# Four edits to the order of work in a hybrid conv/mLSTM decoder block: low weight products one block behind, gate columns first, a merge block in another head, and mean subtractions tile by tile

## The chip, the cores and the metric

The kernel runs on one core of a Trainium2 chip. The core has a matrix engine (TensorE, PE in the profile), whose weight loads the profile lists apart as PEld, a vector engine (VectorE, DVE), a scalar engine (ScalarE, ACT), a small general engine (GpSimd, POOL) and a sync engine (SyncE, SP) that issues most of the transfers. The engines run side by side, each through its own fixed list of instructions in order, and wait for each other through semaphores.

The metric is the device time of one execution in microseconds (us). The time of the kernel before is the median of three runs, 1705.99 us (1705.5 to 1708.39).

## The reference, cut to what matters

One decoder block over 1024 tokens of width 1024, in float32. A conditioned RMS norm feeds one wide input projection. Its columns go to a gated convolution branch, an mLSTM branch with four heads, and two merge gates per channel. The gated sum goes through an output projection, and a SwiGLU feed-forward network and a last norm follow.

```python
h = rms_norm(x, norm_mix_g[l]) * (1.0 + sc1) + sh1
proj = jnp.einsum("bsd,de->bse", h, w_in[l]) + b_in[l]
glu_in, qk_in, v, o_pre, if_pre, merge_pre = jnp.split(proj, IN_SPLITS, axis=-1)

a = glu_in[..., :CONV_WIDTH] * jax.nn.sigmoid(glu_in[..., CONV_WIDTH:])
a = causal_depthwise_conv(a, conv_dw_w[l], conv_dw_b[l])          # 31 taps
a = jax.nn.silu(layer_norm(a, conv_ln_g[l], conv_ln_b[l]))
y_conv = jnp.einsum("bsc,cd->bsd", a, w_conv_pw[l]) + b_conv_pw[l]

qk = jax.nn.silu(causal_depthwise_conv(qk_in, qk_conv_w[l], qk_conv_b[l]))   # 4 taps
...
hm = mlstm_chunkwise(heads(q), heads(k) * (MLSTM_HEAD_DIM ** -0.5), heads(v),
                     gates[:, :MLSTM_HEADS], gates[:, MLSTM_HEADS:])
...
y_mlstm = jax.nn.sigmoid(o_pre) * hm
g_conv, g_mlstm = jnp.split(jax.nn.sigmoid(merge_pre), 2, axis=-1)
y = jnp.einsum("bsd,de->bse", g_conv * y_conv + g_mlstm * y_mlstm, w_out[l])
x = x + g1 * y
...
x = x + g2 * jnp.einsum("bsf,fd->bsd", jax.nn.silu(gt) * up, w_ffn_down[l])
```

## The kernel before, in words

**Products.** Activations are kept transposed, 128 channels by 1024 tokens per tile. A float32 operand is split into a high part (written by ScalarE in the matmul's own 32-bit type) and a low part (the rest, subtracted by VectorE). A product is then three matmuls: high by high, high weights by low activations, low weights by high activations. One **block** is 128 output columns of a projection over the contraction of 1024, that is, over eight slices k of 128. `mm_k` (L160 to L165) issues, for one k, three products times two halves of 512 tokens: six matmuls, all recorded under L165. A block is 48 of them and writes one accumulator `mm` (two PSUM banks, two such tiles exist). `load_split` loads a block's weights `wraw` (512 KB, issued by SP), splits them into `whi` on ScalarE (L155) and `wlo` on VectorE (L156); each of the three has two buffers. `wblock` runs a block as a generator, one k per step, and `block` runs one at once for the pointwise convolution.

**Who sets the order.** The program is laid out as Python generators; a planner with a timing model then fixes each engine's list, by the program's order as priority, and lets work that is ready in the model pass work that isn't. `tc.high_priority()` moves instructions ahead in that priority. `queue_behind` adds an edge for the planner alone, which keeps one instruction behind another; on one engine it adds no wait at run time. `pump` hands out convolution taps (L395, VectorE, 31 for each of eight channel tiles) from a list `bg`, at a later priority, as credit comes in: each block gives 5500 of credit, a tap costs 1200.

**The stages around the change.** After a prologue (about the first 60 us) the first two gated convolution tiles g0 and g1 are made. For head 0, `v_part(0)` makes the value projection and, in the same matmuls, the eight columns of the input and forget gates: three tiles `wide` (pool tag `t4`, three buffers, shared with the sigmoids of `glu_gate`, `om` and `merge_conv`) hold the high value weights in columns 0 to 255, the high gate columns in 256 to 263 and the low ones in 264 to 271. L583 and L584 write those gate columns from the small load `wif_raw`. Then for each head: `qk_part` (four blocks with a 4-tap convolution on VectorE, L542, each), `v_part`, `decay_mask`, and `mlstm`, a chain over four chunks of 256 tokens that passes from TensorE to VectorE and ScalarE and back at each step and yields 22 times. `mix` weaves other blocks between its steps: `FILL[h]` names them, `NEXT[h]` says how many of their steps go first, and `STEPS[h]` how many follow each step of the chain. There g2 to g7 are convolution tiles (two blocks each), "o" is `om` of the head before (four blocks: two output gates and two merge gates), and m0 and m1 are the first two merge gates of the convolution branch (`merge_conv`, one block each, whose sigmoid is stored to DRAM as `mc_d` by a transfer on ScalarE's queue and loaded again when it is needed).

After head 3 come `om` of head 3, the sum over the channel tiles (`ln_sum`), and the layer norm of the convolution branch (`ln_steps`) woven with the merge blocks m2 to m7, two block steps after each of its steps. `ln_steps` makes the mean on TensorE in two halves of 512 tokens (L839), subtracts it (L844, VectorE, eight tiles times two halves), squares each tile on ScalarE (L846), adds the squares up (L848), and later writes the normalised tiles as `ah` and `al` (L864, L865). The pointwise convolution reads these. It is followed by the output projection, the second norm, and the feed-forward network, whose code the change doesn't touch.

## Time and profile before

| what | us |
|---|---|
| median of the three runs | 1705.99 |
| the profiled execution's own time | 1706.31 |
| its span, first to last instruction | 1704.6 |
| what lies around the span (1706.31 - 1704.6) | 1.71 |
| TensorE busy in the span | 1664.8 |
| VectorE busy in the span | 1310.5 |
| ScalarE busy in the span | 647.5 |

The profile shows one execution, taken by the hardware profiler. The busy time of TensorE counts the time in which at least one matmul is recorded as running. Matmuls are pipelined and their ends are modelled, so two neighbours overlap in the records, and the spacing of their starts tells the pace. A row of the timeline gives the start, the duration, the engine, the line, the operation, the tile written and the tiles read; in brackets stands the idle time of the engine just ahead of the row and what ended it. Rows of windows give the length of each stretch, then each engine's busy time in it with the number of instructions, then the TensorE clock that was granted (1.00 is full), the share of the DMA engines and the rate in GB/s.

### The profile page before, as it was taken

Reading aid. Unit: us, or ns where it says so; the run is one execution under the profiler, and the core shown is the slowest. Engines: PE = TensorE matmul, PEld = TensorE weight load, DVE = VectorE, ACT = ScalarE, POOL = GpSimd, SP = SyncE. Lnnn points to the kernel's source line nnn. Section 1 sums busy time; section 2 is a strip of 40 time slices with the busy share of each in tenths; the row PEclk is TensorE's granted clock in tenths of the full one; section 3 lists DMA queues with packets and bytes.
Section 4 is the critical chain, followed back from the end, with each engine's and each line's share of the span. In section 5 each row is a group of like instructions: output and inputs, shape, how many; then the busy total and the mean of one; then the engine's idle time right before and its main releaser. Section 6 shows DMA issues by size and latency. Waiting matters only on the chain. (4 is left out here: it accounts for less than half of the span.)

```text
span 1704.6 us, 20805 instructions
## 1 busy us (share of the span) xinstructions
PE 1664.8 (98%) x8237; PEld 1394.9 (82%) x8237; DVE 1310.5 (77%) x1760; ACT 647.5 (38%) x835; POOL 59.5 (3%) x116
## 2 busy tenths in 40 slices
PE   5999999999999999999999999999999999999998
PEld 4798888888888889888888778888888888788886
DVE  6989998997699759637699567877767777667776
ACT  7425335322532253224521356422222222344344
POOL 0000001000000000000000000000000000000001
PEclk9999999999999999999999999999999999999999
DMA  9221121122112211224497543333332333495872
GB/s 325 64 63 49 38 62 38 50 62 75 38 39 73 62 38 50 75 82 155 129 374 283 189 160 130 112 105 100 99 104 93 101 98 110 144 355 188 283 248 110
DMA packets 221241, 211.12 MB, mean 124 GB/s; under 512 B 8455, under 2 KB 175127, under 8 KB 221143
## 3 DMA queue, kind: packets, MB, share of 16 engines
q1 hardware_dynamic: 202327, 164.70, 31.3%
q10 hardware_dynamic: 18576, 44.31, 6.9%
q8 instruction: 64, 1.05, 0.3%
q0 software_dynamic: 240, 0.79, 0.1%
q14 instruction: 34, 0.28, 0.0%
HBM read 168.60 MB, written 41.16 MB: 123 GB/s over the span
## 5 line engine op out<-in xcount | busy, mean ns | idle before, releaser
L395 DVE SCALAR_TENSOR_TENSOR cacc<-a,col,cacc 128x1024 f32<-128x1024 f32 x240 | 306.1, 1282 | 3.9 <-ACT cacc L393 1.4
L165 PE MATMUL mm<-hh,wlo 128*128 128x512 f32 x864 | 271.2, 391 | 1.6 <-DVE wlo L156 1.6
L165 PE MATMUL mm<-hl,whi 128*128 128x512 f32 x864 | 272.5, 392 | 0.0
L165 PE MATMUL mm<-hh,whi 128*128 128x512 f32 x864 | 271.6, 392 | 0.0
L165 PEld LDWEIGHTS mm<-hh,wlo 128*128 128x128 f32 x864 | 160.4, 188 | 33.7 <-DVE wlo L156 2.8
L165 PEld LDWEIGHTS mm<-hl,whi 128*128 128x128 f32 x864 | 161.0, 188 | 32.1 <-issue 0.5
L165 PEld LDWEIGHTS mm<-hh,whi 128*128 128x128 f32 x864 | 160.5, 188 | 31.6
L155 ACT ACTIVATE whi<-wraw 128x1024 fp32r<-128x1024 f32 x61 | 64.7, 1060 | 227.4 <-PE mm L165 176.1
L156 DVE TENSOR_TENSOR wlo<-wraw,whi 128x1024 fp32r<-128x1024 f32 x61 | 74.3, 1219 | 28.7 <-ACT whi L155 25.2
L1123 PE MATMUL mm<-Bh,gh 128*128 128x512 f32 (+1 forms) x192 | 71.5, 375 | 2.8 <-ACT gh L1060 1.4
L1124 PE MATMUL mm<-Bl,gh 128*128 128x512 f32 (+1 forms) x192 | 71.5, 373 | 0.7 <-DVE Bl L1042 0.7
L611 PE MATMUL mm<-wlo,hh 128*128 128x256 f32 x256 | 72.0, 282 | 0.0
L1125 PE MATMUL mm<-Bh,gl 128*128 128x512 f32 (+1 forms) x192 | 71.2, 371 | 0.0
L1215 ACT ACTIVATE wd<-reg 128x1024 fp32r<-128x1024 f32 (+1 forms) x36 | 35.2, 988 | 82.6 <-DVE reg L1339 54.2
L542 DVE SCALAR_TENSOR_TENSOR cacc<-qkraw,col,cacc 128x1024 f32<-128x1024 f32 x48 | 61.5, 1281 | 4.9 <-ACT cacc L540 4.5
L1366 PE MATMUL mm<-wd,xl 128*128 128x512 f32 (+1 forms) x154 | 59.6, 387 | 1.2 <-DVE xl L1347 1.2
L1365 PE MATMUL mm<-wd,xh 128*128 128x512 f32 (+1 forms) x154 | 59.6, 387 | 0.0
L1367 PE MATMUL mm<-wd,xh 128*128 128x512 f32 (+1 forms) x154 | 59.5, 386 | 0.0
L610 PE MATMUL mm<-whi,hh 128*128 128x256 f32 x192 | 54.5, 284 | 0.0
L612 PE MATMUL mm<-whi,hl 128*128 128x256 f32 x192 | 54.2, 283 | 0.0
L1347 DVE TENSOR_TENSOR xl<-xr,xh 128x1408 fp32r<-128x1408 f32 x27 | 43.7, 1619 | 8.7 <-ACT xh L1346 8.7
L1216 DVE TENSOR_TENSOR wd<-reg,wd 128x1024 fp32r<-128x1024 f32 (+1 forms) x36 | 40.2, 1132 | 11.2 <-ACT wd L1215 11.0
(501 smaller groups left out, 3863.8 us busy)
## 6 DMA issues: line engine op xcount, KB each, us to landing
wraw<-in_w_in_dram SPq DMA_DIRECT2D x64, 512.0 KB
xr<-act_d SPq DMA_DIRECT2D x27, 704.0 KB
awt<-in_w_ada_dram SPq DMA_DIRECT2D x32, 512.0 KB
graw<-in_w_ffn_up_dram SPq DMA_DIRECT2D x24, 512.0 KB
act_d<-cg ACTq DMA_DIRECT2D x48, 256.0 KB
uraw<-in_w_ffn_up_dram SPq DMA_DIRECT2D x22, 512.0 KB
reg<-in_w_ffn_down_dram SPq DMA_DIRECT2D x20, 512.0 KB
other<-in_w_ffn_down_dram SPq DMA_DIRECT2D x20, 512.0 KB
```

What stands on the lines that cost most here:

```text
L155: nc.scalar.activation(hi, raw, AF.Copy)
L156: (eng or nc.vector).tensor_sub(lo, raw, hi.bitcast(F32))
L165: nc.tensor.matmul(flat(acc)[:, a:b], lhs[:, k, :], rhs[k][:, a:b], start=(first and k == 0), stop=(last and k == kt - 1))
L395: nc.vector.scalar_tensor_tensor(acc, a[:, j:j + S], dw_col(j, ct), acc, op0=OP.mult, op1=OP.add)
L542: nc.vector.scalar_tensor_tensor(cv, raw[:, j:j + S], wcol(j), cv, op0=OP.mult, op1=OP.add)
L611: nc.tensor.matmul(o[:, 0:256], hh[k][:, ts_], los[k], start=False, stop=False)
L1123: nc.tensor.matmul(o, a, rh, start=(k == 0), stop=False)
L1124: nc.tensor.matmul(o, a, rl, start=False, stop=False)
L1125: nc.tensor.matmul(o, b, rh, start=False, stop=(k == 3))
L1365: nc.tensor.matmul(o, xh, wh, start=(k == 0), stop=False)
L1366: nc.tensor.matmul(o, xl, wh, start=False, stop=False)
L1367: nc.tensor.matmul(o, xh, wl, start=False, stop=(k == FP - 1))
```

## The change

Four edits, none of which changes what is computed or how many matmuls there are.

1. `mm_k` issues the two matmuls with the low weights of slice k after the four with the high weights of slice k+1. In the last slice, those of k=6 and k=7 both follow. This holds for all blocks that go through `wblock` and `block`.
2. In `v_part(0)` the writes of the gate columns are put at high priority.
3. The merge block m1 moves from the fill of head 3 to the end of the fill of head 0, and head 0's pace goes from 1.8 to 2.1 block steps for each step of its chain.
4. In `ln_steps` the sixteen subtractions of the mean are kept in the program's order: both halves of tile 0, both of tile 1, and so on.

```diff
-STEPS = (1.8, 2.8, 2.8, 2.8)
+STEPS = (2.1, 2.8, 2.8, 2.8)
...
     def mm_k(acc, k, kt, w, xh, xl, parts=HALVES):
         hi, lo = w
-        for lhs, rhs, first, last in ((hi, xh, True, False), (hi, xl, False, False), (lo, xh, False, True)):
+        steps = [(hi, xh, k), (hi, xl, k)]
+        if k:
+            steps.append((lo, xh, k - 1))
+        if k == kt - 1:
+            steps.append((lo, xh, k))
+        for i, (lhs, rhs, j) in enumerate(steps):
             for a, b in parts:
-                nc.tensor.matmul(flat(acc)[:, a:b], lhs[:, k, :], rhs[k][:, a:b],
-                                 start=(first and k == 0), stop=(last and k == kt - 1))
+                nc.tensor.matmul(flat(acc)[:, a:b], lhs[:, j, :], rhs[j][:, a:b],
+                                 start=(k == 0 and i == 0), stop=(i == 3))
...
-                nc.vector.tensor_copy(t[:, 0:n, 256:264], wif_raw[:, ks])
-                nc.vector.tensor_sub(t[:, 0:n, 264:272], wif_raw[:, ks], t[:, 0:n, 256:264].bitcast(F32))
+                with tc.high_priority():
+                    nc.vector.tensor_copy(t[:, 0:n, 256:264], wif_raw[:, ks])
+                    nc.vector.tensor_sub(t[:, 0:n, 264:272], wif_raw[:, ks], t[:, 0:n, 256:264].bitcast(F32))
...
-    FILL = ("g2 g3 m0", "g4 o g5", "g6 o g7", "o m1")
+    FILL = ("g2 g3 m0 m1", "g4 o g5", "g6 o g7", "o")
...
         ssum = t4()
+        before = None
         for ct in range(8):
             for i in range(2):
-                nc.vector.tensor_sub(halves(cv[ct], i), halves(cv[ct], i), mean[i])
+                ins = nc.vector.tensor_sub(halves(cv[ct], i), halves(cv[ct], i), mean[i])
+                if before:
+                    queue_behind(ins, before)
+                before = ins
```

## The prediction

> **What bounds the kernel now.** The first view is the page's head: TensorE is busy 98% of the span. The second is the table of windows over stages, whose first figure after each stretch's length is TensorE's busy time.
>
> ```profile
> span 1704.6 us, 20805 instructions
> PE 1664.8 (98%) x8237; PEld 1394.9 (82%) x8237; DVE 1310.5 (77%) x1760; ACT 647.5 (38%) x835; POOL 59.5 (3%) x116
> ```
>
> ```profile
> 0.00:60.00 60.00, 42.19 (x194) 33.52 (x195) 46.47 (x73) 43.54 (x68) 2.74 (x8) 0.94 0.78 250
> 60.00:860.00 800.00, 795.32 (x4245) 683.83 (x4244) 644.92 (x842) 297.52 (x361) 40.24 (x89) 1.00 0.23 68
> 860.00:1100.00 240.00, 231.52 (x1204) 193.85 (x1203) 188.41 (x298) 102.14 (x154) 5.50 (x8) 1.00 0.60 206
> ```
>
> The change keeps every matmul, so it can win only idle time of TensorE. Its edits lie between 60 and 860 us, from the work ahead of head 0 to the end of the layer norm; only the blocks of the pointwise convolution, which edit 1 touches too, run on after that. There TensorE idles 800.00 - 795.32 = 4.7 us. The prologue (17.8 us) and the stage from 860 to 1100 (8.5 us) idle more, but no wait there is one of an edited line. The third view is the list of TensorE's waits in that stretch: what waited, what released it, us in total, times, the longest.
>
> ```profile
> PE pc L636 <- DVE kwl L684: 1.8, 1, 1.8
> PE mm L165 <- DVE wlo L156: 1.6, 2, 0.9
> PE mm L610 <- DVE t L584: 0.6, 1, 0.6
> PE pa L132 <- DVE col L135: 0.4, 1, 0.4
> PE pc L634 <- ACT kwh L683: 0.3, 1, 0.3
> ```
>
> That is 4.7 us, the whole idle time, in six waits. The first three kinds and the last belong to edits 3, 1, 2 and 3.
>
> These idle times are too small, since a matmul's modelled end lies after the start of the next. The pace is in the windows of L165 alone:
>
> ```profile
> 160.00:268.20 108.20, 98.39 (x406) 73.86 (x404) 1.00 0.20 58
> 268.20:274.40 6.20, 0.00 (x0) 0.00 (x0) 1.00 0.33 85
> 608.00:636.00 28.00, 28.00 (x124) 22.92 (x123) 1.00 0.15 39
> 660.30:769.60 109.30, 91.61 (x381) 69.88 (x382) 1.00 0.28 85
> 769.60:791.20 21.60, 21.59 (x95) 17.73 (x95) 1.00 0.52 180
> ```
>
> From 608 to 636 us blocks run alone: 28.00 / 124 = 0.226 us from start to start, and a block of 48 takes 10.8 us. I therefore size each wait by starts.
>
> **Edit 2, gate columns first.** The timeline at the wait:
>
> ```profile
> 87.32 1.28 DVE L395 SCALAR_TENSOR_TENSOR cacc<-a,col,cacc 128x1024 f32<-128x1024 f32 x1
> ...
> 87.87 0.28 PE L611 MATMUL mm<-wlo,hh 128*128 128x256 f32 x1
> 87.98 0.29 PE L612 MATMUL mm<-t,hl 128*128 128x272 f32 x1
> 88.52 0.17 DVE L584 TENSOR_TENSOR t<-wif_raw,t 128x16 fp32r<-128x16 f32 x1
> ...
> 88.83 0.36 PE L610 MATMUL mm<-t,hh 128*128 128x272 f32 x1 [0.56 <-DVE t L584]
> ```
>
> A write of 0.17 us sits behind a convolution tap of 1.28 us. TensorE starts at 88.83 instead of 87.98 + 0.11 (the spacing of the two starts above it): 0.74 us. Moved ahead of the tap, the write would end by about 87.5, before it is needed. Six small writes change place, and no load does. If one of them now reaches the head of VectorE's list before its load or its tile is there, the taps behind it wait, which TensorE doesn't need here. I take -0.7; the bounds are -0.74 and 0.
>
> **Edit 1, low products one block behind.** The two waits for `wlo`:
>
> ```profile
> 302.38 0.63 PE L165 MATMUL mm<-hl,whi 128*128 128x512 f32 x2
> ...
> 302.63 1.22 DVE L156 TENSOR_TENSOR wlo<-wraw,whi 128x1024 fp32r<-128x1024 f32 x1
> ...
> 303.90 0.72 PE L165 MATMUL mm<-hh,wlo 128*128 128x512 f32 x2 [0.90 <-DVE wlo L156]
> ...
> 481.82 0.63 PE L165 MATMUL mm<-hl,whi 128*128 128x512 f32 x2
> 481.91 1.22 DVE L156 TENSOR_TENSOR wlo<-wraw,whi 128x1024 fp32r<-128x1024 f32 x1
> ...
> 483.18 0.73 PE L165 MATMUL mm<-hh,wlo 128*128 128x512 f32 x2 [0.74 <-DVE wlo L156]
> ```
>
> Both blocks stand at a head's start, where the split is done about 2 us late. By starts the waits are 303.90 - 302.38 - 0.45 = 1.07 and 483.18 - 481.82 - 0.45 = 0.91 us (0.45 is two starts). With four more matmuls ahead of the first low product it is needed 4 x 0.226 = 0.90 us later, so 0.17 and 0.01 us stay and 1.80 go. The number of matmuls and weight loads is unchanged, and the order of weights still runs high k, low, high: the pace should hold. In a block where the split is in time the edit does nothing; its last slice has eight matmuls for six, and the accumulator is complete at the same count. I take -1.8; the bounds are -1.8 and 0.
>
> **Edit 3, m1 in head 0.** The windows of L165 show that blocks fill head 0 until 268.2 us and then none runs for 6.2 us. There the chain is bare:
>
> ```profile
> 269.28 0.28 PE L636 MATMUL pn<-vh,scl 128*128 128x258 f32 x1
> ...
> 269.87 0.38 PE L634 MATMUL pc<-vh,kwh 128*128 128x258 f32 x1 [0.31 <-ACT kwh L683]
> ...
> 270.33 0.28 PE L635 MATMUL pc<-vl,kwh 128*128 128x258 f32 x1
> ...
> 270.65 1.28 DVE L542 SCALAR_TENSOR_TENSOR cacc<-qkraw,col,cacc 128x1024 f32<-128x1024 f32 x1
> ...
> 271.85 0.48 DVE L684 SCALAR_TENSOR_TENSOR kwl<-pa,wsc,kwh 128x256 fp32r<-128x256 f32 x1
> ...
> 272.38 0.50 PE L636 MATMUL pc<-vh,kwl 128*128 128x258 f32 x2 [1.76 <-DVE kwl L684]
> ```
>
> Starts of such narrow matmuls are 0.11 us apart (87.87 and 87.98 above), so the two waits cost 269.87 - 269.28 - 0.11 = 0.48 and 272.38 - 270.33 - 0.11 = 1.94 us. With m1, 48 more matmuls (10.8 us) lie in head 0 and VectorE has as much longer. It gets one more weight split (1.22 us in the rows of edit 1) and 5500 / 1200 = 4.6 more taps of 1.28 us, 7.1 us in all, so it gains 3.7 us on TensorE, twice the larger wait. I take -2.4; the bounds are -2.4 and 0. What m1 brings along is a 512 KB load on SP's queue ahead of later weight loads, a split and a sigmoid on ScalarE, and a 512 KB store on its queue: beside a DMA share of 0.20 between 160 and 268 us these are hidden.
>
> What it takes from head 3: 381 matmuls, almost eight blocks, run there from 660.3 to 769.6 us, and 95 more (two blocks, those of the last `om`) until 791.2. Without m1 the planner can pull one of these two forward, since their matmuls don't need the chain's result. Then head 3 has the same cover, and the stretch between its end and the pointwise convolution is a block shorter. The layer norm, which must be done in that stretch, has this to spare:
>
> ```profile
> 785.60 1.22 DVE L833 TENSOR_TENSOR t4b<-t4b,cv 128x1024 f32<-128x1024 f32 x1
> ...
> 791.26 1.02 PE L839 MATMUL pn<-t4b,ones_d 128*128 128x512 f32 x2
> ```
>
> ```profile
> L165 PE MATMUL mm<-al,whi x128: 392/396/480, 851.5 to 943.0; 128*128 128x512 f32 x128
> L865 DVE TENSOR_TENSOR al<-cv,ah x8: 1216/1219/1226, 838.0 to 855.3; 128x1024 fp32r<-128x1024 f32 x8
> ```
>
> The sum over the tiles is done at 786.8, and the mean's product comes 4.4 us later. The last `al` is done at 855.3 + 1.22 = 856.5; slice k=7 is reached 7 x 6 matmuls of 0.226 us after 851.5, at 861.0, so 4.5 us are left. A block less is 10.8 us against 4.5 + 4.4 of slack and what edit 4 frees. I take nothing lost; the bound above is in the second rival.
>
> **Edit 4, mean tile by tile.** The groups of L844:
>
> ```profile
> L844 DVE TENSOR_TENSOR cv<-cv,pn x8: 678/679/686, 792.3 to 796.5; 128x512 f32<-128x512 f32 x8
> L844 DVE TENSOR_TENSOR cv<-cv,pc x8: 676/677/678, 797.1 to 801.3; 128x512 f32<-128x512 f32 x8
> ```
>
> All first halves run before any second half, so ScalarE can square no tile before 797.8. Tile by tile the first tile is whole after two subtractions, at 793.6 and not at 797.8: 4 us more slack for the layer norm. No matmul waits there, so in the sum it is 0. The edge adds no wait at run time; behind a subtraction on VectorE stand only the others and splits of merge blocks. If this cover were gone (with edit 3's shorter stretch), it pays part of that.
>
> **The sum.** 0.7 + 2.4 + 1.8 = 4.9 us. Against it I set 0.7 us for short waits that a newly planned order will have of its own, the size of the two least in the list of waits (0.4 + 0.3). That is -4.2: the profiled execution's 1706.31 (span 1704.6 and 1.71 around it) goes to 1702.1. The median of the runs shown is 0.32 us less, and so the forecast is 1701.8.
>
> **The rivals.** First, the waits move. VectorE is the cause of most of them: a split or a weighted key stands behind taps, and a new plan can put it there again, in head 0 or in head 3, whose own list is now only one `om`. Then the 2.4 comes back: 1701.8 + 2.4 = 1704.2. For it speaks that the chain of head 0 waits in just the place where no block is left; against it that two blocks of the last `om` can be pulled into head 3.
>
> Second, and slower: the block taken out of head 3 is missed as cover for the layer norm. If the planner pulls a block forward and the mean's product doesn't move up, the pointwise convolution starts 10.8 us earlier and finds `al` 10.8 - 4.5 = 6.3 us late; if the slack is used up too, 10.8. An idle stretch that long would also cost clock. In the prologue, where TensorE is busy 42.19 of 60 us, the windows have a stretch at half clock (the 0.50):
>
> ```profile
> 29.20:35.90 6.70, 5.03 (x12) 4.01 (x13) 6.44 (x9) 5.00 (x7) 0.00 (x0) 0.50 1.09 348
> ```
>
> Half of 5.03 is 2.5 us lost; the waits of up to 1.94 us between 60 and 860 left it at 1.00. So this rival costs 8.8 to 13.3, less the 4.9: 1709.9 to 1714.4, say 1711. It decides from 4.9 + 3.4 = 8.3 us on. [...]
>
> Third, edit 1 doesn't do what it says: the planner sees that the low part is wanted 0.90 us later and lets a tap (1.28 us) go first. Then the 1.8 stays: 1703.6. Against it: taps are queued at a later priority already.
>
> **How the numbers follow.** Forecast 0.58, waits that move 0.22, edit 1 without effect 0.09, layer norm uncovered 0.11. What a measurement of this kernel can tell from no change is about 0.2%, 3.4 us: faster is below 1702.6, slower above 1709.4. Of the forecast's 0.58, 0.05 lies just short of that bound, so faster has 0.53, same 0.05 + 0.22 + 0.09 = 0.36, slower 0.11. The stage after 860 us, whose code doesn't change, is planned anew as well, and one of its waits could go or come:
>
> ```profile
> PE mm L1123 <- ACT mm L1020: 1.3, 1, 1.3
> ```
>
> The range begins at 1699.8: 1706.0 less 4.9 and less such a wait. It ends at 1708.6: no edit gains (their upper bounds), the 0.7 us of short waits come, and head 3 has a wait like head 0's 1.9. Only the slow rival lies outside.
>
> **What would show it.** Right: TensorE's waits between 60 and 860 us below 1.5 us in all, none for `t` of L584, none for `kwl` in head 0, those for `wlo` gone or below 0.2; L165 filling the gap of 6.2 us in head 0; the L844 rows alternating between the two halves; the pace still 0.226. Wrong: a wait of the chain of head 3 (L634 to L636), a wait for `al` or `ah` at the first pointwise block, a slice with a clock below 1.00, or a longer idle time after 860 us, which I hold unchanged.

## The result, and the profile after

The changed kernel takes 1714.63 us (median of 6 runs, 1714.04 to 1719.82) where the kernel before takes 1706.26 us beside it: a ratio of 1.0054, 95% interval 1.0039 to 1.0069. It is slower by about 8 us; the forecast was 4 us faster, and its range ended at 1708.6.

The head of the page of the changed kernel, and its windows over the stages (the columns are those of the kernel before):

```profile
span 1712.4 us, 20822 instructions
...
PE 1665.6 (97%) x8237; PEld 1394.6 (81%) x8237; DVE 1311.3 (77%) x1760; ACT 649.6 (38%) x835; POOL 60.6 (4%) x116
```

```profile
60.00:860.00 800.00, 793.18 (x4236) 681.85 (x4235) 639.48 (x833) 298.62 (x361) 41.34 (x89) 1.00 0.23 68
860.00:1100.00 240.00, 228.27 (x1171) 191.33 (x1170) 190.11 (x299) 101.40 (x152) 5.52 (x8) 0.99 0.60 205
```

TensorE's idle time between 60 and 860 us went from 4.7 to 800.00 - 793.18 = 6.8 us, and between 860 and 1100 from 8.5 to 11.7 us, where the granted clock now is 0.99. The list of TensorE's waits says which: first from 60 to 860 us, then the four largest from 860 to 1100 (a line number of the changed kernel is 5 to 10 above the old one: L170 is the old L165, L775 the old L769, L875 the old L865, L1016 the old L1006).

```profile
PE mm L170 <- DVE al L875: 3.7, 2, 2.9
PE mm L170 <- ACT t4b L775: 1.9, 1, 1.9
PE mm L616 <- DVE t L590: 0.6, 1, 0.6
PE pa L132 <- DVE col L135: 0.4, 1, 0.4
PE mm L170 <- ACT ah L874: 0.3, 1, 0.3
...
PE pa L1022 <- ACT whi L1016: 3.2, 1, 3.2
PE mm L1024 <- DVE wlo L1017: 2.2, 1, 2.2
PE pa L1133 <- DVE su L1157: 1.8, 1, 1.8
PE mm L1133 <- ACT gh L1070: 1.7, 1, 1.7
```

The waits for `kwl`, `kwh` and `wlo` are gone, as the change meant. In their place stand waits of the layer norm (`t4b`, `ah`, `al`: 5.9 us) and longer ones of the output projection (5.4 us, before 2.3). Of the waits that the edits were aimed at, only the one for the gate columns, 0.6 us, is where it was.

By the starts of the first or last matmuls of each stage, in one profiled execution of each:

| stretch | before, us | after, us | difference |
|---|---|---|---|
| up to the last transpose of head 3 | 769.58 | 775.41 | +5.8; less the 10.8 us of m1: -5.0 |
| from there to the output projection's first matmul | 174.58 | 170.44 | -4.1; plus the 10.8 us of m1: +6.7 |
| output projection | 93.82 | 98.84 | +5.0 |
| from there to the down projection's first matmul into `mm` | 450.05 | 451.57 | +1.5 |
| the rest | 216.57 | 216.09 | -0.5 |

So the heads won the 5 us that they were to win. The layer norm took 6.7 back, and the output projection, in which no line was edited, 5.0. In the 1.5 us behind it the waits sum to about the same (6.1 us before, 6.2 after), but the clock is at 0.50 for 3.4 us from 1087.7 on, behind a wait of 1.8 us; in the kernel before it is not below 1.00 anywhere in that stretch.

**Where the layer norm's time is.** The groups of the mean's subtraction, the normalising multiplication and `al` in the changed kernel (duration min/median/max in ns, first and last start in us):

```profile
L851 DVE TENSOR_TENSOR cv<-cv,pn x8: 677/680/687, 798.4 to 807.0; 128x512 f32<-128x512 f32 x8
L851 DVE TENSOR_TENSOR cv<-cv,pc x8: 676/678/687, 799.2 to 807.6; 128x512 f32<-128x512 f32 x8
...
L872 DVE TENSOR_TENSOR cv<-cv,pn x8: 677/677/687, 833.2 to 841.6; 128x512 f32<-128x512 f32 x8
L872 DVE TENSOR_TENSOR cv<-cv,pc x8: 676/677/679, 837.4 to 842.2; 128x512 f32<-128x512 f32 x8
...
L875 DVE TENSOR_TENSOR al<-cv,ah x8: 1215/1218/1226, 844.7 to 863.0; 128x1024 fp32r<-128x1024 f32 x8
```

The subtractions alternate now, and the multiplications of the next loop (L872) still run seven first halves ahead of any second half. But the mean's product starts at 797.33, 21.9 us after head 3's end (before: 21.7), and the last `al` starts 87.6 us after it (before: 85.8). The layer norm hangs on head 3's end and didn't get shorter, while the blocks beside it became one fewer (292 matmuls of L170 behind head 3's end, before 339 of L165). Nor did the alternating subtractions bring the next step forward. The additions of the squares, after and before:

```profile
L858 DVE TENSOR_TENSOR t4b<-t4b x7: 1214/1225/1226, 809.4 to 818.4; 128x1024 f32<-128x1024 f32 x7
```

```profile
L848 DVE TENSOR_TENSOR t4b<-t4b x7: 1216/1225/1225, 803.0 to 812.0; 128x1024 f32<-128x1024 f32 x7
```

The last of them starts 21.1 us after the mean's product (before: 20.7), and TensorE's product for the variance 27.1 us after it (before: 27.2). The timeline of TensorE at the first pointwise block and of ScalarE and TensorE at the mean:

```profile
799.96 1.06 ACT L856 ACTIVATE t4b<-cv 128x1024 f32<-128x1024 f32 x1 [1.33 <-DVE cv L851]
...
800.93 1.10 ACT L775 ACTIVATE t4b<-mm,col 128x1024 f32<-128x1024 f32 x1
...
802.08 0.73 PE L170 MATMUL mm<-hh,whi 128*128 128x512 f32 x2 [1.94 <-ACT t4b L775]
...
852.74 0.74 PE L170 MATMUL mm<-al,whi 128*128 128x512 f32 x2 [0.80 <-DVE al L875]
...
857.30 0.73 PE L170 MATMUL mm<-al,whi 128*128 128x512 f32 x2 [2.89 <-DVE al L875]
```

By starts these waits are 2.1 us at the mean (a merge block needs an accumulator whose sigmoid stands behind the first square on ScalarE) and 0.4 + 1.0 + 3.1 = 4.5 us at the pointwise convolution: 6.6 us.

**Where the projection's time is.** Its weight loads are issued by SP; the groups of that line in the changed kernel and, after the "...", who waited for it (us, times), and then the same of the kernel before:

```profile
L1015 SPq DMA_DIRECT2D wraw<-in_w_out_dram x16: 367/368/6093, 913.2 to 1023.6; - x16
...
  ACT whi L1016: 11.3, 3
```

```profile
L1005 SPq DMA_DIRECT2D wraw<-in_w_out_dram x16: 367/368/2199, 912.7 to 1016.8; - x16
...
  ACT whi L1006: 0.6, 1
```

One issue took 6.1 us instead of 0.4, and ScalarE's splits waited 11.3 us for loads. The timeline of TensorE there:

```profile
973.56 0.39 PE L1024 MATMUL pc<-wlo,y 128*128 128x512 f32 x1
977.10 0.50 PE L1022 MATMUL pa<-whi,y 128*128 128x512 f32 x1 [3.16 <-ACT whi L1016]
...
978.69 0.63 PE L1022 MATMUL pc<-whi,y 128*128 128x512 f32 x1
979.12 0.63 PE L1023 MATMUL pc<-whi,y 128*128 128x512 f32 x1
```

After the wait (3.3 us by starts) come matmuls that start 0.43 us apart (978.69 and 979.12) instead of 0.23: half clock (granted clock 0.50 from 978.48 to 981.89), seven of them, 1.4 us. Together with the second wait (2.4 us by starts; the two were 1.4 and 1.2 us before) and four transposes that ran ahead of the projection before (0.4 us), this is nearly all of the projection's 5.0 us.

### The profile page after: what moved, and what is told of

It is laid out like the page before. It is cut to its first block, busy times and chain, and to the rows that moved or that the text cites. A ratio compares the mean times of both kernels' runs of the same rounds, so it can differ in the third digit from the quotient of the medians.

```text
span 1712.4 us, 20822 instructions
## 1 busy us (share of the span) xinstructions
PE 1665.6 (97%) x8237; PEld 1394.6 (81%) x8237; DVE 1311.3 (77%) x1760; ACT 649.6 (38%) x835; POOL 60.6 (4%) x116
## 5 line engine op out<-in xcount | busy, mean ns | idle before, releaser
L170 PE MATMUL mm<-hh,whi 128*128 128x512 f32 x864 | 271.2, 391 | 1.9 <-ACT t4b L775 1.9
L170 PE MATMUL mm<-hl,whi 128*128 128x512 f32 x864 | 271.5, 391 | 0.0
L170 PE MATMUL mm<-hh,wlo 128*128 128x512 f32 x864 | 262.3, 391 | 0.0
L170 PEld LDWEIGHTS mm<-hh,whi 128*128 128x128 f32 x864 | 160.7, 188 | 34.0 <-ACT t4b L775 2.4
L170 PEld LDWEIGHTS mm<-hh,wlo 128*128 128x128 f32 x864 | 160.5, 188 | 32.2 <-issue 0.5
L170 PEld LDWEIGHTS mm<-hl,whi 128*128 128x128 f32 x864 | 160.5, 188 | 31.1
L617 PEld LDWEIGHTS mm<-wlo,hh 128*128 128x128 f32 x256 | 48.6, 190 | 0.0
```

Source lines behind the costliest of these rows:

```text
L170: nc.tensor.matmul(flat(acc)[:, a:b], lhs[:, j, :], rhs[j][:, a:b], start=(k == 0 and i == 0), stop=(i == 3))
L617: nc.tensor.matmul(o[:, 0:256], hh[k][:, ts_], los[k], start=False, stop=False)
```

## The experiments

Four theories go through the expectations. **A**: m1 was the layer norm's cover, and the loss stands there. **B**: any new plan moves waits about in the stages behind, whatever was edited. **C**: edit 4 puts a square ahead of a merge block's sigmoid on ScalarE. **D** and later **X** are on the projection: D that the loads of x stand in front of a weight split on ScalarE's queue, X that these loads leave too late and what they bring then collides with the weight loads. "Front" is the start of the output projection's first matmul. All kernels in one table, us; the last column but one, "x leaves", is the start of the first load of x, counted from the projection's first matmul, and "rest" is what follows the projection:

| kernel | median | ratio to before, 95% | front | projection | x leaves | rest |
|---|---|---|---|---|---|---|
| before | 1706.26 | 1 | 944.2 | 93.8 | 7.5 | 666.6 |
| after | 1714.63 | 1.0054 (1.0039 to 1.0069) | 945.9 | 98.8 | 11.7 | 667.7 |
| no_m1 | 1707.01 | 1.0002 (0.9992 to 1.0011) | 942.8 | 93.8 | 7.3 | 671.8 |
| only_m1 | 1712.90 | 1.0034 (1.0021 to 1.0047) | 950.1 | 93.3 | 7.8 | 668.4 |
| only_low | 1705.59 | 0.9991 (0.9981 to 1.0000) | 942.3 | 94.7 | 6.3 | 666.3 |
| no_mean | 1709.24 | 1.0010 (1.0001 to 1.0019) | 948.2 | 94.6 | 7.7 | 665.3 |
| hold | 1710.16 | 1.0020 (1.0010 to 1.0031) | 946.3 | 93.2 | 6.2 | 669.6 |
| x_behind | 1715.34 | 1.0054 (1.0037 to 1.0070) | 945.7 | 98.4 | 11.7 | 667.1 |
| x_first | 1711.49 | 1.0027 (1.0014 to 1.0041) | 947.2 | 95.4 | 9.4 | 667.2 |
| mul_order | 1709.41 | 1.0012 (1.0003 to 1.0021) | 942.5 | 98.1 | 14.5 | 670.3 |
| ln_pull | 1710.59 | 1.0020 (1.0010 to 1.0029) | 948.0 | 93.4 | 7.6 | 667.4 |
| ln_both | 1713.86 | 1.0037 (1.0022 to 1.0051) | 950.9 | 95.5 | 6.3 | 664.5 |
| mo_x | 1715.07 | 1.0041 (1.0028 to 1.0053) | 944.1 | 99.1 | 14.6 | 670.1 |
| mo_x_gates | 1713.65 | 1.0034 (1.0022 to 1.0045) | 944.4 | 98.0 | 14.6 | 669.6 |
| mo_x_mean | 1703.70 | 0.9974 (0.9965 to 0.9984) | 939.4 | 96.7 | 9.9 | 666.9 |
| low_gates | 1704.97 | 0.9983 (0.9974 to 0.9991) | 941.5 | 95.1 | 6.3 | 667.6 |
| mean_only | 1712.81 | 1.0032 (1.0020 to 1.0044) | 945.4 | 100.2 | 11.7 | 667.1 |
| mo_mean | 1706.21 | 0.9993 (0.9985 to 1.0002) | 939.2 | 100.2 | 11.8 | 666.7 |
| mo_mean_gates | 1708.19 | 1.0004 (0.9995 to 1.0013) | 940.6 | 98.4 | 11.8 | 666.2 |

Each ratio is to runs of the kernel before on the same chip (1706.3 to 1707.8 us); front, projection and rest are from one profiled execution. That execution can lie some 3 us from its kernel's median (no_m1 3.1 and mul_order 3.2 above, x_behind 2.5 below), so a difference of that size in one column alone shows little.

### One part undone, or one alone

**no_m1** is the changed kernel without edit 3, **only_m1** the kernel before with edit 3 alone, **only_low** the kernel before with edit 1 alone, **no_mean** the changed kernel without edit 4. Each takes or leaves one hunk of the diff above, the first two this one:

```diff
-STEPS = (2.1, 2.8, 2.8, 2.8)
+STEPS = (1.8, 2.8, 2.8, 2.8)
...
-    FILL = ("g2 g3 m0 m1", "g4 o g5", "g6 o g7", "o")
+    FILL = ("g2 g3 m0", "g4 o g5", "g6 o g7", "o m1")
```

no_m1, expected: 

> Edits 1, 2 and 4, with m1 left in head 3. Theory A (the moved block was the layer norm's cover, and the longer waits of the output projection come with it): no wait for al or for t4b at the pointwise convolution (6.5 us in the changed kernel), the output projection's waits as before (1.2 us for whi, not 3.2), the wait for kwl in head 0 back (2.4), those for wlo gone (-1.8): about 1704.5. Theory B (any new plan disturbs the output projection, whatever edit causes it): the same, but 3 to 5 us more there, about 1708.5.

only_m1, expected: 

> Edit 3 alone. Theory A: head 0's wait for kwl gone (-2.4), the layer norm late by 6 us or more, since the mean is not taken off tile by tile, the output projection 3 to 5 us longer: 1713 to 1717. Theory B: the layer norm late, the output projection as it falls, 1710 to 1714. Theory C (edit 4 puts a square ahead of a merge block's sigmoid on ScalarE, and that is the 2.1 us wait for t4b): no wait for t4b here.

only_low, expected: 

> Edit 1 alone. Theory A: the two waits for wlo go, all else stays: 1704.5, and the stage after 860 us idles 8.5 us as before. Theory B: the new plan adds 3 to 5 us to the output projection: 1708 to 1709.5.

no_mean, expected: 

> Edits 1, 2 and 3 without edit 4. If edit 4 helps the layer norm by the 4 us by which the first square can start earlier: waits for al and t4b of 6.5 to 10.5 us, 1714.6 to 1718.6. If the plan fixes the layer norm's pace whatever the order of the subtractions: 6.5 us, 1714.6. Theory C: the 2.1 us for t4b is gone, 1712.5.

Without edit 3 the change is at the old kernel's time, and with edit 3 alone it is 0.34% slower: the moved block carries most of the loss. Its front alone is 6.0 us late, of which 1.6 arise in the prologue. Several expectations were missed. no_m1 lies between its two values: the projection is short, as A said, but a wait of 0.9 us for `wlo` stayed, and the rest is longer. In only_m1 the layer norm is late, as A said, but the projection is no longer than before (93.3), against A. no_mean is below all three of its values, 5.4 us faster than the changed kernel. So edit 3 or edit 4 taken out gives back most of the 8 us, and among these kernels only the one with both has the long projection; edit 4 alone was not run. The one wait of the layer norm in no_mean (without edit 4), on the timeline:

```profile
803.78 1.06 ACT L852 ACTIVATE t4b<-cv 128x1024 f32<-128x1024 f32 x1 [5.26 <-DVE cv L850]
804.75 1.10 ACT L775 ACTIVATE t4b<-mm,col 128x1024 f32<-128x1024 f32 x1
...
805.89 1.22 PE L170 MATMUL mm<-hh,whi 128*128 128x512 f32 x2 [5.86 <-ACT t4b L775]
```

The square stands ahead of the sigmoid here too, and it waits for the first tile's second half, which comes behind eight first halves. Theory C falls: edit 4 doesn't cause that wait, it shortens it from 5.9 to 1.9 us (5.6 in only_m1, also without edit 4). Edit 4 is worth 2.3 us of front (948.2 against 945.9), though I had costed it at 0; but the plan with it has a projection that is 4.2 us longer, and in total it loses. In only_low this wait for a low part is still there, the other is gone:

```profile
PE mm L170 <- DVE wlo L156: 0.9, 1, 0.9
```

Alone, edit 1 shortens the front by 1.9 us, though only half of it by the waits that it was aimed at; the wait for `kwl` in head 0 fell by 0.7 us besides. The wait that stayed is not a new tap's: VectorE has a tap and then the split, as before (the split starts at 302.78, before at 302.63), but TensorE begins the block 0.8 us sooner (301.00, before 301.82), and that uses up the room which the four matmuls gave.

### The block kept behind head 3

**hold**: the changed kernel, with the last block of `om` of head 3 (the one that the planner had pulled into head 3 in m1's place) and the blocks behind it kept behind the head's last transpose.

```diff
+            if e == 7:
+                hold.append(turns[-1])
             pm = yield from wblock(MM0 + e * 128)
...
+                if hold and k == 0 and i == 0:
+                    queue_behind(ins, hold[0])
```

> The changed kernel, with the last block of head 3's om kept on TensorE behind the last transposes of head 3's chain, so that the layer norm has the cover of seven blocks again that it had before. Theory A (the block pulled into head 3 is the layer norm's missing cover): the waits for t4b and al (6.5 us) go, and the pointwise convolution begins without a wait; if head 3's chain needs the block as much, waits of up to 6 us for kwl, scl or Cl come there instead. Without such waits 1708, with them 1714. If the layer norm is late for its own work (edit 4's order on VectorE and ScalarE), the 6.5 us stay.

The layer norm's waits vanished, and one of nearly the same size came up in the head, on the list of waits:

```profile
PE pa L757 <- DVE num L750: 4.9, 1, 4.9
```

The total, 1710.2 us, lies between the two expected values, because this plan's projection is short again (93.2). So the block is cover in one place or the other. Head 3 needs eight blocks beside it, the layer norm the rest, and with m1 in head 0 there is one too few for both. That is theory A, shown from both sides.

### The loads of x

**x_behind** (theory D) keeps the fifth and sixth load of x behind a weight split, so that the split goes first:

```diff
-        nc.scalar.dma_start(x, x2[t * 128:(t + 1) * 128, :])
+        ins = nc.scalar.dma_start(x, x2[t * 128:(t + 1) * 128, :])
+        if t in (4, 5):
+            queue_behind(ins, splits[4])
```

> The changed kernel, with two loads of x (the fifth and sixth on ScalarE's queue) kept behind one weight split of the output projection; all else in the plan up to there is the same. Theory D (the output projection waits longer because in the new plan these two loads sit in front of the split and wait 5.8 us for a transfer that used the same queue slot before them): the split comes at about 961 instead of 966, TensorE's wait of 3.3 us falls to 1.5 or less and the half clock after it goes: 3 to 5 us less than the changed kernel, about 1710. If the split is late for another reason (its load, or TensorE's own delay of 2 us): 1714, unchanged.

The split came 3.4 us sooner (962.7 instead of 966.1), and the wait stayed at 3.1 us. D falls. The next split, which TensorE waits for, again stood for its load.

**x_first** (theory X) does the opposite with an earlier split:

```diff
-            nc.scalar.activation(hi, raw, AF.Copy)
+            ins = nc.scalar.activation(hi, raw, AF.Copy)
+            if (q, eh, kk) == (0, 0, 3):
+                queue_behind(ins, x_loads[3])
```

> The changed kernel with all four edits, and the fourth weight split of the output projection queued on ScalarE behind the fourth load of x, so that these four loads leave ahead of it as they do in the kernel before. Theory X (the loads of x leave 11.7 us after the projection's first matmul where the others have 6.2 to 7.8, and the bulk that they bring then collides with the weight load that came 3.3 us late): the projection goes from 98.8 us back to about 94, no wait over 2 us in it, no matmuls at the half clock, 1710 to 1711 us. Theory B (any new plan moves the waits about): a wait of about 3 us stays somewhere in it, 1712 to 1716 us.

The loads left 2.3 us sooner, the projection took 3.5 us less, and the total 3.1 less (the intervals of the two ratios overlap by a little). That supports X in its main line; a wait of 2.3 us with eight matmuls at half clock stayed (granted clock 0.81 from 975 to 980 us, 0.85 from 980 to 985), which X did not expect. The front is 1.4 us longer than in the changed kernel with nothing changed in it: the same 3.1 us wait for `al` was followed by half clock this time (granted clock 0.75 from 857.2 to 864.0 us, in the changed kernel 1.00).

The table says the same over all kernels. Where x leaves within 8 us, the projection takes 93.2 to 95.5 us (nine kernels); at 9.4 and 9.9 us 95.4 and 96.7; at 11.7 us or later 98.0 to 100.2 (eight kernels). Two things limit what this shows. First, x is late for a reason of its own: the loads stand behind the copy `mrow` in ScalarE's list, and `mrow` needs the transposes of `aacc`, a task in the background. In the ten kernels where x leaves after 9 us, four or eight of these run behind the projection's first matmul; in the other nine none does. Second, a slow issue is not enough to lengthen the projection: only_low, low_gates and ln_both have one of 8.3 to 8.4 us and projections of 94.7 to 95.5, while mul_order has none above 0.4 us and takes 98.1, with a wait of 3.8 us for `wlo`. So late loads mark the long projections, but how they lengthen them is not shown in every kernel.

### The layer norm made shorter

**mul_order** keeps the normalising multiplications tile by tile as edit 4 does for the mean. **ln_pull** holds merge blocks behind the mean, the variance and the row factors, at the steps at which the trace shows their operands ready (the second diff shows the mean alone). **ln_both** has both.

```diff
+        before = None
         for ct in range(8):
             for i in range(2):
-                nc.vector.tensor_mul(halves(cv[ct], i), halves(cv[ct], i), rows[i])
+                ins = nc.vector.tensor_mul(halves(cv[ct], i), halves(cv[ct], i), rows[i])
+                if before:
+                    queue_behind(ins, before)
+                before = ins
```

```diff
+                if turn and turn[0] in held:
+                    queue_behind(ins, held.pop(turn[0]))
...
-            nc.tensor.matmul(mean[i], ones_d, halves(csum, i), start=True, stop=True)
+            held[13] = nc.tensor.matmul(mean[i], ones_d, halves(csum, i), start=True, stop=True)
```

mul_order: 

> The changed kernel with all four edits, and the sixteen multiplications by the row factors of the layer norm kept in program order too, tile by tile, as edit 4 does for the subtractions. In the changed kernel the first silu of the layer norm waits for the eighth multiplication. Theory A (the layer norm's latency ends last at the pointwise convolution): the first silu starts some 3 us sooner, the wait of 3.06 us for the last low part goes, and with it the two shorter ones: front 3 to 4.5 us shorter, 1710 to 1712 us. Theory B (the plan after it decides): front the same or shorter, the rest longer, 1714 us or more.

ln_pull: 

> The changed kernel with all four edits, and the merge blocks' matmuls held behind the mean (from their 13th step of six matmuls, counted from 0), the eight matmuls of the variance (from the 28th) and the transposes of the row factors (from the 31st): TensorE takes these three as soon as the trace shows their operands ready instead of 4.7, 4.7 and 5.1 us later. Theory A: the layer norm ends 10 us or more sooner, every wait of the pointwise convolution's first block goes, front 4 to 6.5 us shorter (939 to 942 us to the output projection's first matmul), 1708 to 1711 us. Theory B: front shorter, but the rest longer than the 766.5 us it has, 1712 us or more.

ln_both: 

> The two edits on the layer norm together. Theory A: no more than the better of the two alone (the layer norm is then off the path with room to spare): front 939 to 941 us, 1707 to 1710 us by the mean of the stretch after it (762 us over the kernels so far). Theory B: as with either alone, and the stretch after it anywhere between 760 and 767 us.

In mul_order the first silu starts at 834.42, where the changed kernel has it at 840.25:

```profile
833.10 0.69 DVE L873 TENSOR_TENSOR cv<-cv,pn 128x512 f32<-128x512 f32 x1 [6.79 <-PE pn L869]
833.71 0.68 DVE L873 TENSOR_TENSOR cv<-cv,pc 128x512 f32<-128x512 f32 x1
...
834.42 2.44 ACT L877 ACTIVATE cv<-cv,col 128x1024 f32<-128x1024 f32 x2 [7.58 <-DVE cv L873]
```

The waits at the pointwise convolution shrank from 4.5 to 0.7 us, the front by 3.4 us and the total by 5, to just below the expected range: A. ln_pull and ln_both missed their fronts by 6 us and more; that ln_pull's total fell into A's range is due to its short projection. The pull took the mean's wait away, but the planner set other things in the way: a split of a merge block's low part behind the layer norm's work (3.3 us, ln_pull), or the first pointwise block ahead of a merge block's matmuls, behind that block's accumulator (7.2 us, ln_both).

### Together

**mo_x** joins mul_order and x_first. **mo_x_mean** adds the pull of the mean alone (`held[13]`); **mo_mean** is that without x_first, **mean_only** the pull alone. **mo_x_gates**, **mo_mean_gates** and **low_gates** (edit 1 and the gate columns) replace edit 2 by this:

```diff
+    wif_hi = hp.tile([128, KT, 8], F32R, name="wif_hi")
+    nc.vector.tensor_copy(wif_hi, wif_raw)
+    nc.vector.tensor_sub(wif_raw, wif_raw, wif_hi.bitcast(F32))
...
-                    nc.vector.tensor_copy(t[:, 0:n, 256:264], wif_raw[:, ks])
-                    nc.vector.tensor_sub(t[:, 0:n, 264:272], wif_raw[:, ks], t[:, 0:n, 256:264].bitcast(F32))
+                    nc.scalar.activation(t[:, 0:n, 256:264], wif_hi[:, ks].bitcast(F32), AF.Copy)
+                    nc.scalar.activation(t[:, 0:n, 264:272], wif_raw[:, ks], AF.Copy)
```

mo_x: 

> The changed kernel with all four edits, the multiplications of the layer norm tile by tile, and the fourth weight split of the output projection behind the loads of x: the two orders that each won back about 3 to 5 us alone, together. Theory A+X (the two losses are separate and are what made the change slower): front as with the multiplications alone, 942.5 us, projection about 94.5 to 95.5 us, the rest 667 to 669 us: 1704 to 1707 us. Theory B (a shorter wait in one place is paid by a longer one in another): 1709 us or more.

mo_x_mean: 

> As the kernel with both orders, and the mean's matmuls ahead of the merge blocks' 13th step, 3.6 us sooner, as in the kernel that pulled mean, variance and row factors; the other two are left to the planner. Theory A: the 2.11 us wait at the sigmoid behind the square goes and the last wait for a low part too: front 2.5 to 3 us shorter than with both orders (939.5 to 940 us). Theory B: a weight split of a merge block is put behind the layer norm's work, as in that kernel (3.33 us wait for a low weight tile), and the front is no shorter.

mean_only: 

> The changed kernel with all four edits and the mean's matmuls ahead of the merge blocks' 13th step, nothing else. Theory A (the layer norm's latency is what the lost block uncovered, so starting it 3.6 us sooner pays the same wherever the planner's slack is taken out): the 2.11 us wait behind the square goes, of the three waits for ah and al (4.5 us) at most 1 us stays, front about 940 us, 6 us less than with the four edits. Theory B: the front stays above 944 us, because the planner moves a weight split or the first block in the way, as when all three were pulled.

mo_mean: 

> The fastest kernel so far (1703.7 us) without the order of the loads of x. No edit acts ahead of the output projection that differs, so the front is 939.4 us again. Theory X (the time at which the loads of x leave sets the projection's length): with x leaving within 8 us of the projection's first matmul it takes about 94 us, with 11 us or more about 98 us; the total follows, 1701 or 1705 us.

mo_x was a miss: 1715 us. The two edits that each won 3 to 5 us did not add up. Its timeline shows the loads of x behind `mrow`, a small copy that waits for two transposes which this plan runs only 14 us into the projection; the weight split that I had tied to these loads came late with them:

```profile
958.22 0.38 PE L960 MATMUL pa<-ident,modc 128*8 128x128 f32 x2
...
958.63 0.37 ACT L961 ACTIVATE mrow<-pa 8x256 f32<-8x256 f32 x1 [7.05 <-PE pa L960]
...
958.72 3.92 ACTq L1009 DMA_DIRECT2D x<-in_x_dram  x4
...
963.84 0.50 PE L1029 MATMUL mm<-whi,y 128*128 128x512 f32 x1 [2.06 <-ACT whi L1021]
```

An edge can hold the split back; it can't bring the loads forward. mo_x_mean has `mrow` at 949.20 and the loads at 949.28, and there the same edge paid. Its window from 60 to 860 us, the group of its weight loads and its longest wait in the projection:

```profile
60.00:860.00 800.00, 798.77 (x4263) 687.25 (x4262) 644.15 (x839) 301.87 (x363) 41.27 (x89) 1.00 0.23 69
...
L1027 SPq DMA_DIRECT2D wraw<-in_w_out_dram x16: 368/368/1542, 907.5 to 1015.0; - x16
...
PE pa L1036 <- ACT whi L1028: 3.5, 1, 3.5
```

From 60 to 860 us TensorE idles 1.2 us, the layer norm's waits are gone, the front is 939.4 us: 4.7 us under the kernel before. No split waits for a weight load, though TensorE still waits 3.7 us (by starts) for one, with eight matmuls at half clock behind it (granted clock 0.99 from 860 to 1100 us). mo_mean has the same front without the edge, and its longest issue of these loads is 8.7 us:

```profile
L1026 SPq DMA_DIRECT2D wraw<-in_w_out_dram x16: 368/368/8664, 907.2 to 1018.3; - x16
...
  ACT whi L1027: 11.4, 2
```

That pair supports X: one edge, 1.9 us between the loads (9.9 against 11.8), 3.5 us of projection, and the same transposes in it. 1.2 of the 3.5 us are half clock behind mo_mean's second wait, which goes with the edge (granted clock from 860 to 1100 us: 0.98 in mo_mean, 0.99 in mo_x_mean); the intervals of the two ratios lie just apart. mean_only shows that the mean's place alone is not enough (front 945.4, so B; it still waits for `ah` and `al`). With both orders and the mean pulled, the four edits give 1703.7 us, 0.9974 of the kernel before: the version furthest ahead of both kernels, and the only one by more than 0.2%.

mo_x_gates: 

> As the kernel with both orders, and in place of edit 2 the gate columns are split once, early, into two small tiles, and ScalarE copies them into the wide tiles when their slots come free (no subtraction that waits for a cast). If the 0.72 us wait at 88 us comes from the tap that runs between cast and subtraction, it goes: head 0 ends 0.7 us sooner (299.8 us) and the total is 0.7 us less than with both orders, or more or less by what the new plan does behind it. If the wait comes from the free slot alone, it stays at 0.5 to 0.7 us.

low_gates: 

> Edit 1 with the gate columns split early and copied by ScalarE; no edits 3 and 4. Against edit 1 alone (1705.6 us, ratio 0.9991): if the tap between cast and subtraction makes the gate wait, 0.7 us less in head 0, about 1705 us and a ratio near 0.9987; the stretch after the output projection's first matmul has no edit and may differ by up to 3 us from its 761.0 us all the same (theory B).

mo_mean_gates: 

> As that, with the gate columns split early in place of edit 2. In the two kernels with it the wait at 85 to 88 us stayed, for the accumulator that the gated product of tile 1 frees. So no gain in the front beyond 0.3 us (939.1 to 939.7 us); the total as without it, give or take the 3 us by which the stretch behind it varies.

Why edit 2 moved nothing is on VectorE's timeline of the changed kernel: the cast goes first, and a weight split and a tap still run between it and the subtraction, in the very order of the kernel before (there 86.64, 86.72, 87.32 and 88.52). The likely reason is that the planner doesn't take the subtraction for ready yet; no run tests that.

```profile
86.71 0.17 DVE L589 CAST t<-wif_raw 128x16 fp32r<-128x16 f32 x1
...
87.39 1.27 DVE L400 SCALAR_TENSOR_TENSOR cacc<-a,col,cacc 128x1024 f32<-128x1024 f32 x1
88.59 0.16 DVE L590 TENSOR_TENSOR t<-wif_raw,t 128x16 fp32r<-128x16 f32 x1
```

With the split made early no subtraction is left there, and TensorE waits all the same, in low_gates:

```profile
84.69 1.28 DVE L405 SCALAR_TENSOR_TENSOR a<-mm,col,t 128x1024 f32<-128x1024 f32 x1
...
86.02 0.39 PE L617 MATMUL mm<-vb_two,ones_v 128*128 128x272 f32 x1 [0.60 <-DVE a L405]
```

The gated product of tile 1 frees an accumulator only then. In this plan it starts at 84.69; in the changed kernel it started at 83.71, and TensorE did not wait for it. So the early split removed one wait and its plan brought another, 0.8 to 1.6 us by starts in the three kernels. mo_mean_gates, where it is longest, missed its front (940.6). Whether a subtraction that really runs ahead of the tap would win the 0.7 us is not shown. That the ratio of low_gates is 0.0008 below that of only_low lies within their intervals.

## Why the prediction was wrong, step by step

- **Edits 1 and 3, "-1.8" and "-2.4":** right together. Up to head 3's end 5.0 us went (4.2 forecast), with `kwl`, `kwh` and both `wlo` waits. Edit 1 alone keeps one of the two. That has the price of the third rival, but not its mechanism: no tap came first, the block began sooner.
- **Edit 2, "-0.7":** 0. The step that failed is "moved ahead of the tap, the write would end by about 87.5". It ended at 88.75, behind the same tap: the subtraction hangs on the cast, and the raised priority left the order as it was.
- **Edit 3's cover, "I take nothing lost":** this step failed, for 6.7 us. The second rival had the mechanism: the planner pulled a block forward, the mean's product did not move up, `al` was 6.3 us late by forecast and the layer norm 6.6 by measurement. That these agree so well is partly luck: 4.5 us stand at the pointwise convolution and 2.1 at the mean, behind a sigmoid that the rival doesn't name. I had counted 4.4 us between the sum and the mean's product, and edit 4's 4 us, as slack. But the planner put the mean no sooner after the head's end (21.9 us), and edit 4's 4 us were gone before the variance: its product comes 27.1 us after the mean's, as before. That the order of the next loop (L872), which no edit touched, costs 3.4 us of front is what mul_order shows. Of the rival's price, the clock loss wasn't paid in the layer norm (1.00 there) but in the projection (1.4 us).
- **Edit 4, "in the sum it is 0":** without it the layer norm costs 2.3 us more of front. In the new plan a matmul does wait at that place, for a sigmoid behind the square, and "4 us more slack for the layer norm" did not reach its end: the last `al` starts 87.6 us after head 3's end with edit 4 and without it.
- **The stage after 860 us, "which I hold unchanged", and "0.7 us for short waits":** the largest failure beside the layer norm, 6 us in all. The projection has 5.0 of it, in longer waits (3.0), half clock (1.4) and moved transposes; with it the loads of x left 4.2 us later, and two pairs of kernels show that their order against a weight split is worth 3.5 us. Why this plan put them late is followed back only to the transposes of `aacc`. The 1.5 us of the feed-forward stage go with a stretch at half clock (0.50 for 3.4 us from 1087.7 on); without any edit there, the rest varies from 664.5 to 671.8 us over the profiled executions, and why stays open.
- **What would show it:** the L844 rows alternate, the pace held, the `kwl` and `wlo` waits are gone; and of the signs against it, the wait for `al` at the first pointwise block, a clock below 1.00 and the longer idle time after 860 us all came.

The size of 1711 us that I gave the second rival was the layer norm and its clock alone. The forecast's other fault is in the chances: 0.11 for the layer norm, and nothing for a loss behind it.

## What to carry to other kernels

A block of independent work that fills a bare wait is taken from somewhere: before it is moved, ask for each stretch that loses it what latency it covered, and count as slack only what the plan is known to use. Where a planner lays out the whole program, a small edit also moves work it doesn't touch: set an allowance from the size of the longest waits in the later stages (here 3 to 5 us), and check the time at which the big transfers leave, not only who waits. And before a wait is priced by moving one instruction ahead, look at what that instruction itself hangs on (here the subtraction on its cast).

## What the runs showed of the hardware

- Waits of TensorE of 2 to 3 us were followed by half clock in some executions and by full clock in others. The wait at the mean, 2.1 us by starts in the changed kernel, in the windows of the changed kernel and of mo_x (the sixth figure after the stretch's length is the granted clock):

```profile
799.00:802.00 3.00, 1.14 (x5) 0.56 (x3) 2.83 (x6) 2.04 (x3) 0.00 (x0) 1.00 0.00 0
802.00:804.00 2.00, 1.93 (x8) 1.61 (x9) 2.00 (x4) 2.00 (x4) 0.00 (x0) 1.00 0.57 229
804.00:806.00 2.00, 2.00 (x10) 1.68 (x9) 2.00 (x5) 2.00 (x3) 0.00 (x0) 1.00 0.08 33
```

```profile
799.00:802.00 3.00, 1.07 (x5) 0.54 (x3) 2.83 (x6) 2.10 (x3) 0.00 (x0) 1.00 0.00 0
802.00:804.00 2.00, 2.00 (x5) 1.63 (x6) 2.00 (x5) 2.00 (x3) 0.00 (x0) 0.54 0.61 246
804.00:806.00 2.00, 2.00 (x7) 1.55 (x7) 2.00 (x5) 2.00 (x3) 0.00 (x0) 0.61 0.04 16
```

  TensorE is idle for 1.9 us of these seven in both. In the two windows behind the wait stand eight and ten matmuls at a granted clock of 1.00, five and seven at 0.54 and 0.61. The wait for the last `al`, 3.1 us by starts, was followed by 1.00 in the changed kernel and by 0.75 in x_first (857.2 to 864.0 us in both). In the changed kernel a wait of 2.4 us at 1003.9 was followed by 1.00 (981.95 to 1020.00), one of 1.8 us by 0.50 (1087.70 to 1091.10), and the one of 3.3 us in the projection by 0.50 (978.48 to 981.89). Behind the 4.9 us for `num` in hold the clock was 0.50 from 770 to 772 us, behind the 5.9 us for `t4b` in no_mean 0.50 from 805.8 to 808.0. Why it fell after some of the shorter waits and not after others is not shown.
- A transfer's issue on SP took up to 8.7 us for the projection's weights in mo_mean, where the median is 0.37 us. In the changed kernel the issue of 6.1 us starts at 960.66, behind four loads of x issued from 957.57 on and two of the feed-forward weights issued at 958.62 and 959.10; the DMA share is 1.01 while it lasts (960.66 to 966.75). mo_x_mean has the same loads, and none of its issues of the projection's weights takes more than 1.5 us.
